# Quadrant swap of a large matrix: four copies on one DMA queue in place of 71 on two

## The chip, the cores and the metric

One core of a Trainium2 chip runs the kernel. The metric is device time in microseconds, the median of several executions. The kernel computes nothing: it moves data from one DRAM tensor to another with the core's 16 DMA engines. Two instruction engines, SyncE (SP) and ScalarE (ACT), issue the copies; each has a DMA queue of its own, and both queues feed the same 16 DMA engines.

## The reference

The input is a matrix of 8192 x 8192 floats (268.44 MB). The result has both halves of both axes exchanged:

```python
def setup_inputs():
    return {"x": np.random.randn(8192, 8192).astype(np.float32)}

def reference(x):
    return np.fft.ifftshift(x)
```

With even sizes this swaps quadrants: row r, column c of the output is row (r + 4096) mod 8192, column (c + 4096) mod 8192 of the input. A row is 32 KiB, half a row 16 KiB, and a half row is the longest piece that is contiguous in both tensors.

## The kernel before

Every copy goes straight from `x` to `out`, by the helper `copy` (lines 26 to 32): it works out the source address from the output's row and column and calls `dma_start` at line 29, so all DMA issues bear that line. `R` and `C` are 8192, `hr` and `hc` 4096.

The access pattern of a copy is `[[step, count], ...]` in elements, outermost first. `back` (line 45) is `[[C, 16], [-16*C, 16], [1, hc]]`: 16 neighbouring rows outermost, one for each DMA engine; then 16 steps (`per`) of 16 rows towards lower rows; then a half row of 16 KiB. One such copy moves 256 rows (`rows`) by half a row, 4 MiB, with 16 packets of 16 KiB on each engine.

The loop (lines 47 to 54) goes through the matrix from its last 1024 rows to its first, in eight groups of four blocks of 256 rows. For each block SP issues the left half (columns 0 to 4095 of the output, line 49) and ACT a right half (columns 4096 to 8191, line 54). ACT takes the blocks of a group in another order, `(n + 2) % 4` (line 50), so the two queues work two blocks, 512 rows, apart.

Ahead of the loop ACT issues seven small copies (lines 36 to 42). They move the right half of one group of 16 rows, in the block that begins at row `start`, in four strips of 1024 columns (4 KiB). Three strips are cut in two copies of k and 16 - k rows, with k = 14, 9 and 4; the fourth is one copy of 16 rows. So the DMA engines with low numbers get more of these 4 KiB pieces than those with high numbers. The block at `start` is then copied with `rest` (line 46), one step of 16 rows short, at line 52.

That makes 32 copies on SP's queue and 39 on ACT's. The framework gives each copy one of eight completion semaphores in turn, and a copy that takes a semaphore for the second time waits until the copy that had it before has landed. As the two queues take turns in the loop, each has up to four copies outstanding. At the end of the kernel SP waits for all of them.

Of the kernel before, what the change touches and what calls it, by code (L numbers as in the profile page):

```python
# [1 line left out]

# [4 lines left out]


ENGINES = 16


@with_exitstack
def kernel(
    ctx: ExitStack,
    tc: tile.TileContext,
    x: bass.AP,
    out: bass.AP,
):
    nc = tc.nc
    R, C = x.shape  # L20
    hr = R // 2
    hc = C // 2
    per = 16
    rows = ENGINES * per

    def copy(queue, row, col, dims):

        src = (row + hr) % R * C + (col + hc) % C
        queue.dma_start(
            out=bass.AP(out.tensor, out.offset + row * C + col, dims),  # L30
            in_=bass.AP(x.tensor, x.offset + src, dims),
        )

    start = R - 3 * rows
    strip = hc // 4
    for n, k in enumerate((14, 9, 4)):
        col = hc + n * strip
        copy(nc.scalar, start + rows - ENGINES, col, [[C, k], [1, strip]])  # L40
        copy(nc.scalar, start + rows - ENGINES + k, col, [[C, ENGINES - k], [1, strip]])
    copy(nc.scalar, start + rows - ENGINES, hc + 3 * strip, [[C, ENGINES], [1, strip]])


    back = [[C, ENGINES], [-ENGINES * C, per], [1, hc]]
    rest = [[C, ENGINES], [-ENGINES * C, per - 1], [1, hc]]
    for first in range(R - 4 * rows, -1, -4 * rows):
        for n in (3, 2, 1, 0):
            copy(nc.sync, first + n * rows + rows - ENGINES, 0, back)
            right = first + (n + 2) % 4 * rows  # L50
            if right == start:
                copy(nc.scalar, right + rows - 2 * ENGINES, hc, rest)
            else:
                copy(nc.scalar, right + rows - ENGINES, hc, back)


# [1 line left out]
_INS = ['x']  # L58
_OUTS = [((8192, 8192), 'float32')]


# [23 lines left out]
```

## Time and profile before

| | us |
|---|---|
| median of 3 runs | 821.31 (820.95 to 821.79) |
| span of the profiled execution | 810.9 |
| SP issues its copies, first to last | 0.73 to 706.75 |
| ACT issues its copies, first to last | 0.73 to 715.31 |

The span runs from the first to the last instruction of the profiled execution; what lies around it (start and end of the program) is in the runs' time and not in the span. The page has a line with the busy share of the DMA engines in 40 slices of the span, a line with what they moved in each slice, a table of the DMA queues (q1 is SP's, q10 is ACT's) and a list of DMA issues. The rates by slice, each 20.3 us long:

```profile
GB/s 302 328 335 329 334 333 331 331 335 330 326 331 329 331 335 330 332 332 337 335 336 333 333 337 330 334 335 331 336 331 333 335 334 335 333 330 336 333 338 296
```

A rate here counts each byte once, though it is read and written. One DMA packet is one contiguous piece, here a half row of 16 KiB, a strip of 4 KiB, or the few bytes of a completion.

### The profile page before, as it was taken

To read this page: it belongs to the slowest core of one execution; us is meant where nothing else is said; L and a number is where in the kernel's file an instruction comes from. 1 tells how busy PE (TensorE), PEld (TensorE's weight loads), DVE (VectorE), ACT (ScalarE), POOL (GpSimd) and SP (SyncE) were. 2 spreads that over 40 slices of the span, in tenths; PEclk is the share of its full clock that TensorE was granted. 3 is DMA by queue.
4 is the path that set the end of the run, shared out by engine and by line. 5 is a ranking of instruction groups with operands and counts; after the bars stand their busy time and mean duration, and the time that the engine had idled before them with its cause. 6 is when DMAs were issued, how large, how long until landed. Compare 5 with 4: busy or idle time off the path is not lost. (4 is left out here: it accounts for less than half of the span.)

```text
span 810.9 us, 116 instructions
## 1 busy us (share of the span) xinstructions
POOL 0.2 (0%) x4
## 2 busy tenths in 40 slices
POOL 0000000000000000000000000000000000000000
DMA  9999999999999999999999999999999999999998
GB/s 302 328 335 329 334 333 331 331 335 330 326 331 329 331 335 330 332 332 337 335 336 333 333 337 330 334 335 331 336 331 333 335 334 335 333 330 336 333 338 296
DMA packets 17520, 268.44 MB, mean 331 GB/s; under 512 B 1088, under 2 KB 1088, under 8 KB 1152
## 3 DMA queue, kind: packets, MB, share of 16 engines
q1 hardware_dynamic: 8704, 134.22, 49.7%
q10 hardware_dynamic: 8816, 134.22, 49.6%
HBM read 268.44 MB, written 268.44 MB: 662 GB/s over the span
## 5 line engine op out<-in xcount | busy, mean ns | idle before, releaser
L69 POOL MEMSET const-bfloat16-1.0<- 128x1 bf16 x1 | 0.1, 102 | 0.0
L69 POOL MEMSET const-uint8-127<- 128x1 uint8 x1 | 0.1, 102 | 0.0
L69 POOL MEMSET const-float32-0.0<- 128x1 f32 x1 | 0.1, 99 | 0.2 <-issue 0.2
L69 POOL MEMSET const-float32-1.0<- 128x1 f32 x1 | 0.1, 99 | 0.0
## 6 DMA issues: line engine op xcount, KB each, us to landing
out_dram<-in_x_dram SPq DMA_DIRECT2D x32, 4096.0 KB, 100.9
out_dram<-in_x_dram ACTq DMA_DIRECT2D x31, 4096.0 KB
out_dram<-in_x_dram ACTq DMA_DIRECT2D x1, 3840.0 KB
out_dram<-in_x_dram ACTq DMA_DIRECT2D x1, 64.0 KB, 10.8
out_dram<-in_x_dram ACTq DMA_DIRECT2D x1, 56.0 KB
out_dram<-in_x_dram ACTq DMA_DIRECT2D x1, 48.0 KB
out_dram<-in_x_dram ACTq DMA_DIRECT2D x1, 36.0 KB
out_dram<-in_x_dram ACTq DMA_DIRECT2D x1, 28.0 KB
```

The lines of the kernel that those rows point to most:

```text
L69: nc = _bacc.Bacc("TRN2", target_bir_lowering=False, num_devices=1)
```

## The change

The helper, the seven small copies and the loop go. Four copies are left, one for each quadrant of the output, in the order top left, top right, bottom left, bottom right, all issued by SP. In each, the outermost 16 are again 16 neighbouring rows, one for each DMA engine; an engine then makes 256 steps of 16 rows, now towards higher rows, with a half row of 16 KiB at each.

```diff
-    per = 16
-    rows = ENGINES * per
-
-    def copy(queue, row, col, dims):
-
-        src = (row + hr) % R * C + (col + hc) % C
-        queue.dma_start(
-            out=bass.AP(out.tensor, out.offset + row * C + col, dims),
-            in_=bass.AP(x.tensor, x.offset + src, dims),
-        )
-
-    start = R - 3 * rows
-    strip = hc // 4
-    for n, k in enumerate((14, 9, 4)):
-        col = hc + n * strip
-        copy(nc.scalar, start + rows - ENGINES, col, [[C, k], [1, strip]])
-        copy(nc.scalar, start + rows - ENGINES + k, col, [[C, ENGINES - k], [1, strip]])
-    copy(nc.scalar, start + rows - ENGINES, hc + 3 * strip, [[C, ENGINES], [1, strip]])
-
-    back = [[C, ENGINES], [-ENGINES * C, per], [1, hc]]
-    rest = [[C, ENGINES], [-ENGINES * C, per - 1], [1, hc]]
-    for first in range(R - 4 * rows, -1, -4 * rows):
-        for n in (3, 2, 1, 0):
-            copy(nc.sync, first + n * rows + rows - ENGINES, 0, back)
-            right = first + (n + 2) % 4 * rows
-            if right == start:
-                copy(nc.scalar, right + rows - 2 * ENGINES, hc, rest)
-            else:
-                copy(nc.scalar, right + rows - ENGINES, hc, back)
+    dims = [[C, ENGINES], [ENGINES * C, hr // ENGINES], [1, hc]]
+    for row in (0, hr):
+        for col in (0, hc):
+            src = (row + hr) % R * C + (col + hc) % C
+            nc.sync.dma_start(
+                out=bass.AP(out.tensor, out.offset + row * C + col, dims),
+                in_=bass.AP(x.tensor, x.offset + src, dims),
+            )
```

## The prediction

> **What bounds the kernel now.** I read the page's slices and queue table first, then what the SP queue waited for, then the DMA issues, then windows that I cut around the start, the two places where one queue is alone, and the end. The page says:
>
> ```profile
> POOL 0.2 (0%) x4
> DMA  9999999999999999999999999999999999999998
> DMA packets 17520, 268.44 MB, mean 331 GB/s; under 512 B 1088, under 2 KB 1088, under 8 KB 1152
> q1 hardware_dynamic: 8704, 134.22, 49.7%
> q10 hardware_dynamic: 8816, 134.22, 49.6%
> HBM read 268.44 MB, written 268.44 MB: 662 GB/s over the span
> ```
>
> No engine computes. The 16 DMA engines are busy in all 40 slices, and the packets of q1 (SP's queue, left half) and q10 (ACT's, right half) fill 49.7 + 49.6 = 99.3% of 16 engines' span. So neither issuing nor waiting costs anything in the middle; the time is the bytes over the rate at which packets get through, 268.44 MB each way. The chain of waits holds only four memsets and is of no use here. SP's waits and the issues:
>
> ```profile
> SPq L29 <- DMA out_dram<-in_x_dram: 686.8, 28, 28.4
> out_dram<-in_x_dram SPq DMA_DIRECT2D x32, 4096.0 KB, 100.9
> out_dram<-in_x_dram ACTq DMA_DIRECT2D x31, 4096.0 KB
> ```
>
> SP waits 686.8 us, 28 times, for one of its earlier copies before it may issue the next: 32 - 28 = 4 copies stand in its queue at a time, and one takes 100.9 us to land while the wait between two is at most 28.4 us. The queue is never empty, so that wait has full cover. Last, the windows (span of the window, GpSimd busy, clock, DMA share, GB/s; a packet counts where it starts):
>
> ```profile
> 0.00:2.18 2.18, 0.20 (x4) 1.00 0.03 8
> 2.18:5.00 2.82, 0.00 (x0) 1.00 1.00 366
> 5.00:12.80 7.80, 0.00 (x0) 1.00 1.00 328
> 12.80:18.00 5.20, 0.00 (x0) 1.00 1.02 336
> 18.00:23.80 5.80, 0.00 (x0) 1.00 1.01 328
> 23.80:420.00 396.20, 0.00 (x0) 1.00 1.00 332
> 420.00:805.30 385.30, 0.00 (x0) 1.00 1.00 334
> 805.30:808.00 2.70, 0.00 (x0) 1.00 0.97 322
> 808.00:810.90 2.90, 0.00 (x0) 1.00 0.19 68
> ```
>
> Four of these are the key, since there one queue works alone, which is what the change makes of the whole run. From 2.18 to 5.00 only SP's first copy moves (366 GB/s). From 5.00 to 12.80 ACT adds only small pieces, 256 KB in all up to 16 us (328). From 18.00 to 23.80 SP's first copy has been read out, its second has not begun, and ACT's queue is alone (328). From 805.30 to 808.00 SP is done and ACT finishes (322). With both queues the rate is 332 to 334.
>
> In the packet records a 16 KiB packet takes 611 ns at the least and 786 ns in the mean, and an engine starts its next packet within 5 ns of the last one's end. [...]
>
> **The change part by part.** The sum is made against the profiled execution, whose span is 810.9 us; the median of the runs is 821.31, so 10.4 us lie around the span, and I keep them.
>
> Bytes moved at the full rate: the last window moves 68 GB/s x 2.9 us = 0.20 MB, so 268.24 MB pass from 2.18 to 808.00 us, in 805.8 us, which is 332.9 GB/s.
>
> *One queue for two.* The three windows of one queue after the start have 328, 328 and 322 GB/s over 7.8, 5.8 and 2.7 us: weighted 327.0. With the first window in, it is (16.3 x 327.0 + 2.82 x 366) / 19.12 = 332.8, so nothing lost. I take 327.0, since the long run resembles engines that have run for a while more than the first four packets of each. 268.24 MB / 327.0 GB/s = 820.3 us, 14.5 us more than 805.8. Windows of 7.8 us taken in a row through the middle scatter from 309 to 351 GB/s, so 327 is within what two queues give by chance too; that is why the bounds stay wide. Lower bound of the rate 309 (868.1 us, +62.3), upper 351 (764.2 us, -41.6).
>
> *71 issues become four, 28 waits go.* An issue takes 570 to 578 ns whether it puts one packet on each engine or 16, so four take about 2.3 us at the start beside the first copy: 0. The 686.8 us of waits are covered, as shown: 0. If a copy of 256 packets per engine ramped up in proportion, its start would be later: in the first copy the 16 engines' first packets begin within 0.33 us of each other (2.18 to 2.51), 16 times that is 5.2 us, once. Between 0 and +5.2 I take 0, as the issue does not grow with the packets.
>
> *Fewer completion packets.* 1088 packets under 512 B are the completions, at 9 ns; four copies leave 64. 1024 x 9 ns / 16 engines = 0.6 us off.
>
> *The 64 pieces of 4 KiB and their uneven split go.* They hold 16 rows; engine 0 gets seven pieces and engine 15 one, so the engines work a few quarter rows apart on ACT's queue. A piece takes 159 ns at the least, four 636, against 611 for a whole half row: 0.0 for the mean. The skew is six pieces, about 1.0 us; without it the end moves by between -1.0 and +1.0 us. I take +0.5, as the end now holds one queue in whole packets with nothing smaller beside it.
>
> *Upward instead of downward, and one quadrant at a time.* The distance between engines stays one row (32 KiB) and the step of an engine 16 rows. Now all reads lie in one half of the columns and all writes in the other, in a single group of rows, where before two groups 512 rows apart and both halves were mixed. Windows with one queue alone have just that (downward), so its price is in the 327; for the direction no row exists, and its bounds are the 309 and 351 above. I take 0.
>
> *No window on how far engines drift.* SP's wait now holds every engine within four copies of 16 packets; with 256 packets per copy and no wait nothing in the code does. Within a copy, the completions of the 16 engines come 1.4 us apart for SP's third copy and 2.0 us for its last, so drift did not build over the run. I take 0; the bound is the growth of a free walk, below.
>
> Sum: 810.9 + 14.5 - 0.6 + 0.5 = 825.3 us of span; with 10.4 around it 835.7, say 836.
>
> **The rivals.** *Same:* the queue makes no difference and 332.9 GB/s holds, span 810.8, time 821. For it: packets are back to back on either count of queues and the first window lifts the mean of one queue to 332.8. Against: every later window of one queue lies at or below 328. The Trainium skill (DMA: Bandwidth & Descriptors, Issuing engines are not separate DMA queues) says that DMAs from several engines run on the same 16 DMA engines, and that issuing from several saves only issue time; by that rule the result is this one, 821, and the back-to-back packets here agree with it.
>
> *Much slower:* reads confined to one half of the rows and writes to the other, in one group of 16 rows, load memory unevenly, and the worst windows become the rule: 309 GB/s, 868.1 + 2.2 + 2.9 + 10.4 = 883.6 us. For it: 805.30 to 808.00, pure in that sense, is the lowest of the rows. Against: 18.00 to 23.80, as pure, has 328.
>
> *Drift:* engines part over 1024 packets with nothing to hold them. SP's first copies end 1.5 us apart after some 32 packets of both queues; a free walk grows by the root of 1024/32, to 8.5 us between first and last. The slowest ends half of that behind the mean, some 4 us past the 836: 840. Against it stands that 1.4 us became only 2.0.
>
> *Faster:* engines that start together on 16 neighbouring rows and are fed by one queue alone stay in step and out of each other's way. From 3.10 to 5.00 us they did:
>
> ```profile
> 3.10:5.00 1.90, 0.00 (x0) 1.00 1.01 414
> ```
>
> That is 16 x 16 KiB / 414 GB/s = 633 ns a packet, near the least of 611. It ended when ACT's first pieces came in at 5.03 us, and after the change none come. It decides if the engines keep step past some ten packets. Fully kept it would give 268.24 / 414 = 648 + 15.5 = 663 us; kept for part of the run, the first window's 366 GB/s gives 748, the best window of the middle, 351, gives 780. Against: writes may still have been piling up in buffers, and 10 us later, with hardly anything from ACT, the rate was 328. The Trainium skill (HBM Reference, Specifications (TRN2)) gives a memory domain about 716 GB/s; the page's 662 read and written is 92% of it, and by that rule no more than 358 GB/s each way could last, an estimate of 765 us at best.
>
> **How the numbers follow.** The forecast (one queue costs 1 to 3%, 829 to 850) 0.45; same 0.12; much slower (850 to 900) 0.20; drift 0.05; faster 0.18. What a measurement can tell from no change is 0.2%, 1.6 us. Faster by more: 0.18 and a little of "same", 0.19. Within: 0.10. Slower: 0.45 + 0.20 + 0.05 and a hundredth of "same", 0.71. The predicted time is the forecast's, 836. The range goes up to 884, the price of 309 GB/s, which leaves out 0.06, and down to 812 (268.24 / 812 less 15.5 is 336.8 GB/s, what the better quarter of the middle windows have), which leaves out 0.14 of "faster". The forecast's own range is 829 to 850.
>
> **What would show it.** One row in the queue table with 16,448 packets and close to 99% of 16 engines, so that the loss is in slower packets (mean near 800 ns) and not in idle engines; slices of about 327 GB/s from the third on, the same in all four quadrants; no DMA wait at line 29's successor; a last slice like the one before. An early drop from about 400 to 330 GB/s within the first 10 us would kill "faster" and show that ACT's pieces did not end the good start. A DMA line with 8s long before the end would mean drift or a queue that runs dry. I am wrong if the middle slices have over 333 GB/s, or under 315.

## The result, and the profile after

The changed kernel takes 824.33 us (median of 20 runs, 821.37 to 832.68) beside 822.23 us for the kernel before on the same chip (20 runs, 819.67 to 824.87). The ratio is 1.0034, with a 95% interval of 1.0019 to 1.0049: slower, by 2 to 3 us. The forecast, 836 against 821.31 us, is a ratio of 1.018; a fifth of that increase was measured. Two more comparisons below have the changed kernel at 1.0050 and 1.0058, 4.6 and 4.9 us.

The page of the changed kernel, its slices and queue table:

```profile
span 822.5 us, 47 instructions
DMA  9999999999999999999999999999999999999998
GB/s 294 321 323 326 326 332 325 332 328 327 335 331 325 324 327 333 325 333 329 330 334 327 322 331 323 333 327 327 327 331 335 328 328 332 331 327 325 330 331 278
q1 hardware_dynamic: 16448, 268.44, 99.2%
HBM read 268.44 MB, written 268.44 MB: 653 GB/s over the span
```

One queue fills the engines as fully as two did (99.2% against 99.3%), with no gap between the quadrants. The rate is lower in the first five slices (294 to 326) and in the last (278), and otherwise runs at 329 on average. The kernel before, in its second profile, has 295 in the first slice, 292 in the last and 322 to 336 in the others.

That profiled execution took 824.32 us, so 1.8 us lie around its span, not 10.4. This suggests that the 810.9 us span of before and the 821.31 us median were not of the same speed: the kernel before has a median of 822.23 us in this comparison, and 821.63, 811.42, 811.00 and 810.88 us in the four comparisons below, each on another chip. Ratios are therefore taken within a comparison, between kernels measured on one chip, and for the traces I use a second profile of the kernel before (label before_again, run time 822.17 us), which comes from a chip of about this speed. Windows of that kernel first (span of the window, GpSimd busy, clock, DMA share, GB/s):

```profile
5.00:20.00 15.00, 0.00 (x0) 1.00 1.01 321
20.00:100.00 80.00, 0.00 (x0) 1.00 1.00 330
100.00:400.00 300.00, 0.00 (x0) 1.00 1.00 328
400.00:800.00 400.00, 0.00 (x0) 1.00 1.00 329
816.00:820.40 4.40, 0.00 (x0) 1.00 0.44 160
```

and of the changed kernel:

```profile
3.10:5.00 1.90, 0.00 (x0) 1.00 0.98 414
5.00:20.00 15.00, 0.00 (x0) 1.00 0.99 318
20.00:100.00 80.00, 0.00 (x0) 1.00 1.00 324
100.00:400.00 300.00, 0.00 (x0) 1.00 1.00 329
400.00:800.00 400.00, 0.00 (x0) 1.00 1.00 329
818.00:822.50 4.50, 0.00 (x0) 1.00 0.31 98
```

From 100 to 800 us, seven eighths of the run, the two are alike. In this pair of profiles the difference of the spans, 822.5 - 820.4 = 2.1 us, sits at the two ends. From 20 to 100 us one queue has 324 GB/s against 330: 80 x 6 / 330 = 1.5 us. From 5 to 20 us it is 0.1 us. At the end, the completion packets of the changed kernel's last copy start from 818.1 to 821.4 us with a mean of 819.8, so the slowest engine ends 1.6 us behind the mean; before, those of ACT's last copy start from 817.3 to 819.2, the slowest 0.9 us behind. That is 0.7 us more. Together 2.3 us. The part at the start comes back in the profiles below; the part at the end does not always (in the changed kernel's second profile the slowest engine is 0.9 us behind the mean, as before).

### The profile page after: what moved, and what is told of

It is laid out like the page before. It is cut to its first block, busy times and chain, and to the rows that moved or that the text cites. A ratio compares the mean times of both kernels' runs of the same rounds, so it can differ in the third digit from the quotient of the medians.

```text
span 822.5 us, 47 instructions
## 1 busy us (share of the span) xinstructions
POOL 0.2 (0%) x4
## 2 busy tenths in 40 slices
DMA packets 16448, 268.44 MB, mean 326 GB/s; under 512 B 64, under 2 KB 64, under 8 KB 64
## 3 DMA queue, kind: packets, MB, share of 16 engines
q1 hardware_dynamic: 16448, 268.44, 99.2%
```

## The experiments

All ratios are to the kernel before, measured in the same comparison on the same chip.

**The kernel before again.** No edit.

> The kernel before, unchanged, for a profile whose own time is known. The changed kernel's profiled execution has 1.8 us around its span (824.32 to 822.5), not the 10.4 that I kept. Theory A, the base was a fast execution: the span here is about 820.4 (822.2 less 1.8), packets take some 796 ns in the mean, and the middle rate is 329 GB/s and not 333. Theory B, what lies around the span differs between the two kernels: the span is near 811 again at a time of 822.

821.57 against 821.63 us, ratio 1.0001 (0.9989 to 1.0012); span 820.4 us, packets 794 ns in the mean. Theory A holds: nothing but 1.8 us lies around the span in this kernel either. So the first profile of before was of an execution of some 812.7 us, which fits the chips on which this kernel takes 811 us, and its middle rate of 333 GB/s must not be set beside 329 here.

**Two queues, four copies.** In the changed kernel:

```diff
-            nc.sync.dma_start(
+            queue = nc.sync if col == 0 else nc.scalar
+            queue.dma_start(
```

> The changed kernel with its left quadrants on SP's queue and its right ones on ACT's: four copies of 256 packets per engine, two queues. Theory queue (one queue alone passes packets at a lower rate): as fast as the kernel before, ratio 1.000. Theory ends (the middle rate does not depend on the queues; the changed kernel loses what its engines are apart at the start and end): like the changed kernel, 1.002 to 1.004.

821.95 us, 1.0005 (0.9990 to 1.0021). That is what theory queue expected; copies of 256 packets cost nothing here by themselves, though a second measurement below, on another chip, has 1.0028. From 20 to 100 us it has 330 GB/s, as in the middle.

**One queue, short copies.** In the kernel before, lines 36 to 42 and the `rest` case go, and:

```diff
-                copy(nc.scalar, right + rows - ENGINES, hc, back)
+            copy(nc.sync, right + rows - ENGINES, hc, back)
```

> The kernel before without its small pieces and with all 64 copies of 16 packets per engine on SP's queue, left and right in turn, downward. Theory queue: 1.003 or more, as the changed kernel. Theory length (copies of 256 packets let engines drift, copies of 16 with waits hold them together): 1.000. Theory ends: 1.002 to 1.004, with the 16 engines' last completions some 3 us apart where the kernel before has 1.5.

824.53 us, 1.0043 (1.0021 to 1.0065). Length is refuted, and with it the direction as a large term: downward with 16 packets a copy, one queue is as slow as the changed kernel. Its last completions are 2.1 us apart, no more than two queues have (1.9 in before_again, 2.4 with four copies), and not the 3 us of theory ends. Its windows:

```profile
20.00:100.00 80.00, 0.00 (x0) 1.00 1.00 322
100.00:400.00 300.00, 0.00 (x0) 1.00 1.00 327
400.00:800.00 400.00, 0.00 (x0) 1.00 1.00 329
```

Again the slow stretch is the first one, but here it lasts longer: in windows of 100 us from 100 us on the rates are 324, 327 and then 330 GB/s.

**Without the small pieces.** In the kernel before, lines 36 to 42 and the `rest` case go; both queues stay.

> The kernel before with a full copy in place of the 64 pieces of 4 KiB; two queues, short copies. Theory skew (the uneven pieces put the engines out of step and save some us at the end): 1.001 to 1.003, last completions further apart than 1.5 us. Theory queue: 1.000, as the pieces do not touch the rate. Each theory has the middle at 329 GB/s.

822.60 us, 1.0011 (0.9998 to 1.0025). The pieces are worth about 0.1% or nothing; this can't tell.

**Two queues in the same half.**

```diff
-    for row in (0, hr):
-        for col in (0, hc):
+    for col in (0, hc):
+        for row in (0, hr):
...
-            nc.sync.dma_start(
+            queue = nc.sync if row == 0 else nc.scalar
+            queue.dma_start(
```

> Four copies of 256 packets per engine, the upper quadrant on SP's queue and the lower on ACT's at the same time, first both left quadrants, then both right ones. Two queues, but at any moment all reads lie in one half of the columns and all writes in the other, as in the changed kernel. Theory queue (what costs is that each engine has one queue to take packets from): 1.000 to 1.001, as with the halves on two queues. Theory halves (what costs is that reads and writes each keep to one half): 1.003 or more.

816.03 us beside 811.42, 1.0054 (1.0041 to 1.0067). By the ratio, theory halves. But the trace shows none of the slow start, 333 GB/s from 20 to 100 us. Where its loss lies isn't shown: SP's queue ran out at 809.7 us and ACT's at 811.5, closer together than in the first profile of the kernel before (806.0 and 809.7), and the kernel before was not profiled on this chip. A second measurement (label two_queues_same_half_2) stood beside the halves on two queues (two_queues_four_2):

> Upper quadrant on SP, lower on ACT, first both left, then both right, once more. Theory halves: 1.004 to 1.006, some 0.004 over the one before. Theory ends (its time goes where one queue ends before the other and the engines are apart): both alike, within 0.0015 of each other.

> The four long copies on two queues once more, left on SP and right on ACT, beside the next kernel on the same chip. Theory halves: 1.000 to 1.002, clearly below the next one. If the 1.0005 was that chip's: as the next one, 1.004 or more.

816.23 us, 1.0043 (1.0017 to 1.0069), and 813.96 us, 1.0028 (1.0006 to 1.0050), beside 811.00. The gap is 0.0015, which theory ends allows and which is less than theory halves' 0.004, but the intervals overlap, and both kernels scatter widely there (810.4 to 819.9 and 810.8 to 818.4 us, the kernel before 807.6 to 815.5). Theory halves is not settled by these, and the first measurement's 1.0005 may have been that chip's or chance.

**One queue, mixed halves.**

```diff
-    dims = [[C, ENGINES], [ENGINES * C, hr // ENGINES], [1, hc]]
-    for row in (0, hr):
+    dims = [[C, ENGINES], [ENGINES * C, 2], [1, hc]]
+    for row in range(0, R, 2 * ENGINES):
```

> All on SP's queue in 512 copies of 2 packets per engine, left and right halves of 32 rows in turn, upward. One queue, but both halves are in work at once as soon as engines are two packets apart, and 512 issues of some 0.57 us lie under the transfers (292 us in all). Theory queue: 1.003 to 1.005, as the changed kernel and the short copies on one queue. Theory halves: 1.000. A third case, a queue that runs dry between copies so short: over 1.01 and a DMA share under 0.98 in the middle.

816.49 us, 1.0055 (1.0041 to 1.0068), with

```profile
DMA packets 24580, 268.50 MB, mean 330 GB/s; under 512 B 8192, under 2 KB 8192, under 8 KB 8192
q1 hardware_dynamic: 24576, 268.47, 99.4%
```

on its page. The 512 copies send 8192 completions. At 9 ns on 16 engines these hold the engines for 4.6 us where the kernel before spends 0.6: an estimate of 4.0 of the 5.1 us lost. That they cost as much isn't shown, since the rate from 100 to 800 us (331 and 333 GB/s) is near that of the other kernels on this chip. No slow start (331 GB/s from 20 to 100 us), and the queue does not run dry (99.4% of 16 engines). So the ratio looked like theory queue and the trace shows nothing of it at the start.

**The changed kernel again.**

> The changed kernel once more, for a second profile. Theory start (one queue is slower only until the engines are out of step, in the first 100 us, at some 324 GB/s against 329, and loses 1.5 to 2 us there): the same again, with 329 GB/s from 100 us on, and the ratio again 1.002 to 1.005. Theory chance (the slow start was one execution's): 329 GB/s from 20 us on, and the loss elsewhere, in the middle or the last 6 us.

815.97 us beside 811.42, 1.0050 (1.0037 to 1.0063). Its windows, and below them those of its third profile (label after_3):

```profile
20.00:100.00 80.00, 0.00 (x0) 1.00 1.00 324
100.00:400.00 300.00, 0.00 (x0) 1.00 1.00 333
400.00:800.00 400.00, 0.00 (x0) 1.00 1.00 332
```

```profile
5.00:20.00 15.00, 0.00 (x0) 1.00 1.00 313
20.00:100.00 80.00, 0.00 (x0) 1.00 1.00 328
100.00:400.00 300.00, 0.00 (x0) 1.00 1.00 332
```

Theory start holds in after_again. In after_3 the stretch from 20 to 100 us is weaker than expected (328, where the expectation below says 320 to 326), and the stretch before it is stronger. The middle lies near the 332 and 334 that the kernel before had in its first profile, but that was of another chip. On these two chips the kernel before was not profiled, and of the 4.6 and 4.9 us lost there the start holds only a part; a middle slower by 0.2%, 1.6 us, can't be excluded.

**Engines far apart.**

```diff
-    dims = [[C, ENGINES], [ENGINES * C, hr // ENGINES], [1, hc]]
+    dims = [[hr // ENGINES * C, ENGINES], [C, hr // ENGINES], [1, hc]]
```

> The changed kernel with each engine on 256 rows that follow one another, so that the engines are 8 MiB apart and not 32 KiB. I took 0 for the address pattern since the distance between engines stays one row. If that mattered, this is clearly slower: packets over 900 ns in the mean and 1.1 or more; if the pattern is of no account, 1.003 as the changed kernel.

813.20 us, 1.0039 (1.0014 to 1.0065); 323 GB/s from 20 to 100 us, then 332 and 334. The distance between engines is of no account here, and it does not cure the start. The Trainium skill (DMA: Bandwidth & Descriptors, Latency and other measured facts) reports copies between HBM tensors at half rate where the row pitch is 4 or 8 MiB; engines 8 MiB apart show nothing of it in this copy.

**A start with mixed halves.** One queue throughout; the first 512 rows in copies of 2 packets, then long ones:

```diff
+    pairs = [[C, ENGINES], [ENGINES * C, 2], [1, hc]]
+    for row in range(0, 512, 2 * ENGINES):
+        for col in (0, hc):
...
+    for row, end in ((512, hr), (hr, R)):
+        dims = [[C, ENGINES], [ENGINES * C, (end - row) // ENGINES], [1, hc]]
...
```

> The changed kernel, but the first 512 output rows go in 32 copies of 2 packets per engine, left and right halves in turn; then four long copies as before, all on SP's queue. Theory start (one queue with long copies is slower for its first 100 us, because the engines set out together in one half, and loses some 2 us there): 328 GB/s or the chip's middle rate from 20 us on, and a ratio some 0.002 under the changed kernel's, 1.001 to 1.003. Theory queue (the loss does not come from the start): the same ratio as the changed kernel, 1.0034 to 1.005.

813.75 us beside 811.00, 1.0026 (1.0002 to 1.0051). Its windows:

```profile
20.00:100.00 80.00, 0.00 (x0) 1.00 1.00 332
100.00:400.00 300.00, 0.00 (x0) 1.00 1.00 333
```

The slow start is gone, and does not come back when the long copies take over near 54 us. The interval is too wide to tell the ratios apart. The edit changes two things at once, the length of the first copies and the mixing of halves, so it can't tell which of them cures the start.

**Uneven pieces on the one queue.** The seven small copies of the kernel before, on SP's queue ahead of the long ones:

```diff
+    strip = hc // 4
+    for n, k in enumerate((14, 9, 4)):
+        copy(0, n * strip, [[C, k], [1, strip]])
+        copy(k, n * strip, [[C, ENGINES - k], [1, strip]])
+    copy(0, 3 * strip, [[C, ENGINES], [1, strip]])
```

> The changed kernel, with its first 16 half rows cut in the uneven 4 KiB pieces of the kernel before, ahead of the long copies on the same queue: engine 0 gets seven, engine 15 one. Theory step (the slow first 100 us come from engines that are in step): no slow start, 1.001 to 1.003. Theory halves (they come from reads and writes that keep to one half each, in step or not): slow until 100 us as in the changed kernel, 1.0034 to 1.005.

818.26 us, 1.0078 (1.0052 to 1.0103), and still 325 GB/s from 20 to 100 us. It doesn't test theory step: the last piece was read out at 7.3 us and the first packet of a long copy began at 7.5, so the engines set out together all the same, after

```profile
2.40:10.00 7.60, 0.00 (x0) 1.00 0.46 153
```

which alone loses some 4 us. In the kernel before SP's first copy is under way beside the same pieces, and without them it was not clearly faster or slower.

**Three on one chip.** The changed kernel, the mixed start, and a start on two queues: SP copies the left half as ever, ACT the first 1024 rows of the right half, and then SP is alone.

```diff
+    copy(nc.sync, 0, 0, hr)
+    copy(nc.scalar, 0, hc, 1024)
+    copy(nc.sync, 1024, hc, hr)
+    copy(nc.sync, hr, 0, R)
+    copy(nc.sync, hr, hc, R)
```

> The changed kernel, beside the two below on one chip. Theory start: 20 to 100 us at 320 to 326 GB/s, some 6 to 9 below the same execution's middle, which loses 1.5 to 2.3 us. Theory chance: no such stretch in this third profile.

> The first 512 rows in copies of 2 packets per engine, left and right in turn, then long copies, one queue throughout. Theory start: full rate from 20 us on, and the median 1.0 to 2.5 us below the kernel above. Theory chance: the two medians within 0.5 us.

> The changed kernel, but ACT's queue copies the first 1024 rows of the right half (64 packets per engine) while SP's copies the left; after some 100 us SP is alone with long copies. Theory start: full rate from 20 us on and also after 100 us, when one queue is alone; the median 1.0 to 2.5 us below the changed kernel's. Theory queue (one queue is slower wherever it is alone): full rate until 100 us, then some 0.3% below the two-queue rate to the end, and the median within 1 us of the changed kernel's.

| | us | ratio to before (810.88 us) | 95% interval |
|---|---|---|---|
| changed kernel | 815.75 | 1.0058 | 1.0043 to 1.0073 |
| mixed start | 812.81 | 1.0036 | 1.0013 to 1.0058 |
| start on two queues | 812.52 | 1.0022 | 1.0005 to 1.0039 |

Both starts bring about 3 us, a little more than expected; for the start on two queues the interval is clear of the changed kernel's. The issues and windows of the start on two queues:

```profile
0.73 551.97 SPq L29 DMA_DIRECT2D out_dram<-in_x_dram  x4
0.73 0.66 ACTq L29 DMA_DIRECT2D out_dram<-in_x_dram  x1
```

```profile
20.00:100.00 80.00, 0.00 (x0) 1.00 1.00 332
100.00:400.00 300.00, 0.00 (x0) 1.00 1.00 332
400.00:800.00 400.00, 0.00 (x0) 1.00 1.00 333
```

ACT's one copy landed at 108 us. After it one queue is alone for 700 us at the same 332 and 333. So a single queue is not slower as such; a single queue that sets out with copies of 16 packets or more per engine is slower while it starts. Six profiles are of kernels that set out on one queue without a mixed start: five have 322 to 325 GB/s from 20 to 100 us, the sixth (after_3) 328 and before that, from 5 to 20 us, 313. The eleven others have 328 to 333 from 20 to 100 us, as in their middles. The 15 us ahead of that are no guide by themselves: the mixed start has 317 there in its second profile and 332 in its first.

A measure of the whole start comes from the packet records: take a profile's own rate from 100 to 800 us, and work back from what had been moved by 100 us to the moment at which a copy at that rate would have had to begin. For the kernels that set out on one queue without a mixed start this is 3.9 to 5.0 us (five profiles, after_3 among them with 3.9; the uneven pieces, with their pause, have 9.7), for the eleven others 1.4 to 3.4 us. So the slow start is in each of these profiles and costs some 1 to 3 us. The same working at the end gives 0.7 to 2.0 us against 0.7 to 1.6, no clear difference. On the last chip the cured starts gain 1.4 us (two queues) and 0.6 us (mixed) by this measure, less than half of the 3 us between the medians; where the rest lies, one profile of each can't show.

## Why the prediction was right in sign and wrong in size

*What bounds the kernel* was right: packets back to back, 99.2% of 16 engines, 16,448 packets. That the mean packet came out at 796 ns where "near 800" was expected, and the slices near the expected 327 GB/s, was luck: the kernel before has 794 ns and 329 GB/s on a chip of that speed, so the chip slowed the packets and not the change. Two readings were a little off: the shortest 16 KiB packet takes 608 ns (611 is the most frequent time) and the shortest piece 156, which changes no term; and SP's queue was empty from 18 to 23.8 us, as the prediction's own windows have it, while ACT's queue kept the engines busy.

*One queue for two* is the step that failed: 14.5 us were forecast from one queue's lower rate over the whole run, and the whole change cost 2.1, 4.6 and 4.9 us in three comparisons. In its place the runs show a single queue at the full rate in the middle, and slower only while it starts, by some 1 to 3 us. Two things were wrong with the step's rows. The windows of one queue alone lay before 24 us or in the last 6 us, and I carried their 327 GB/s over 800 us. And I set this 327 against a middle of 332.9 by a difference of 1.8%, although windows of 7.8 us scatter from 309 to 351 in the same profile: the rows could not carry it. In the middle the difference is nil as far as the profiles tell (329 for the changed kernel, 328 and 329 for the kernel before; 332 with two queues and 332 and 333 with one in the start on two queues). The Trainium skill's rule (DMA: Bandwidth & Descriptors, Issuing engines are not separate DMA queues), that issuing from several engines saves only issue time, agrees with this middle; it does not tell of the start.

*The base* was wrong too: of the 10.4 us "around the span", 1.8 are, and the rest fits a faster chip. This hardly moves the forecast as a ratio.

*71 issues become four, 28 waits go*: nothing, as forecast, though not for the reason given. Not every issue of 256 packets per engine is some 0.57 us long. All four together:

```profile
0.73 559.43 SPq L28 DMA_DIRECT2D out_dram<-in_x_dram  x4
```

The first took 0.67 us; the second, third and fourth, issued while earlier copies were still moving, stay in SP's sequencer for 152, 204 and 203 us. Nothing else waits on SP, so they cost nothing here.

*Completion packets*: 64 are left. The records have 9 ns for each, so 0.6 us less of engine time, too little to be seen in the time; the 8192 of the mixed kernel fit this price and do not prove it.

*Pieces and skew*: +0.5 forecast; dropping them from the kernel before measured +1.0 us, with an interval that takes in zero.

*Address pattern and direction*: 0 was right so far as tried; 32 KiB or 8 MiB between engines, upward or downward, all lie at 1.003 to 1.006 on one queue. The direction was changed only together with the length of the copies.

*Drift*: within each of the four copies the engines' completions are 1.4, 2.0, 2.0 and 3.3 us apart, in the second profile 1.7, 1.4, 1.5 and 1.8, in the third 1.9, 3.1, 3.0 and 2.5. No free walk; 0 was right within a us.

*Rival "same"* came closest; the slow start is what it did not count. *Rival "faster"* fell as the text said it would: the changed kernel has 414 GB/s from 3.10 to 5.00 us and 318 right after, with no piece of ACT's to blame. *Rival "much slower"* found no support.

What stays open: why the start is slow (engines in step was not tested cleanly); where the rest of the 4.6 and 4.9 us lies; what the remaining 0.2 to 0.4% of the cured kernels is; and why many of the variants scatter more from run to run (the changed kernel from 821.4 to 832.7 us, short copies on one queue from 821.6 to 831.2, the kernel before from 819.7 to 824.9). No variant tried beat the kernel before.

## What to carry to other kernels

In this kernel, whose DMA engines are full, going from 71 copies on two queues to four on one was worth 0.3 to 0.6%, and what of it the traces could place lay at the start; look there before simplifying. Do not take a rate for a whole run from windows of a few microseconds near its ends: first see how windows of that length scatter in the steady part. And hold a profile's span against the time of its own run, since two chips differed here by more than the change did.

## What the runs showed of the hardware

The kernel before took 821 to 822 us in two comparisons and 811 us in three, 1.3% apart. From 3.1 to 5.0 us the windows of the kernels that start without a pause have 345 to 448 GB/s, and from 5 to 20 us 313 to 334. A packet counts where it starts, which blurs so short a window; with each packet's bytes spread over its own time the first stretch has 364 to 415 GB/s and the second 310 to 331. So the rate falls within some microseconds to near the 326 to 331 GB/s each way of a whole run, below what 16 engines would move with nothing but fastest packets (608 ns for 16 KiB, 431 GB/s). The Trainium skill (HBM Reference, Specifications (TRN2)) gives a memory domain about 716 GB/s; the 651 to 662 read and written over the span stay under it, and the 364 to 415 each way of the first microseconds (728 to 830), which did not last, lie over it. No run here shows whether both tensors lie in one domain.
